# Eight PSUM banks shared out anew: a second score tile for the attention, two banks in place of three for the projections and for the values

## The chip, the cores and the metric

The kernel runs on one core of a Trainium2 chip. The metric is the device time of one execution in microseconds (us). The kernel before took 1664.14 us (median of 3 runs, 1662.96 to 1664.4).

## The reference

One layer of a hybrid decoder on a sequence of 1024 positions with 1024 channels, in float32:

```
z = x @ w_in; u, xl, gl, q, k, v, fg, gate_logits = split(z)
y_s5  = S5 branch of u        (32 groups of 64 complex states, a scan over the sequence, a gate)
y_lru = gelu(gl) * RG-LRU(conv4(xl))                                 (a scan over the sequence)
y_fox = softmax(q k^T / 8 + cum_i - cum_j, causal) v   (8 heads of 64; cum: sum of log forget gates)
x = LN(ALPHA * x + (sum_b sigmoid(gate_b) * (y_b @ w_branch_b)) @ w_out)
x = LN(ALPHA * x + (silu(x @ w_gate) * (x @ w_up)) @ w_down)
```

## The kernel before, in words

A float32 product is made of three matmuls of split operands (a high and a low part, `mm3` at line 119): high by high, high by low, low by high. A projection block of 128 channels by 512 positions is 24 matmuls of 512 columns into one bank of PSUM (`zpart`, line 194).

PSUM has eight banks of 2 KB a partition. Up to the end of the mixing stage one pool holds them, by tag. Tag `b`: one bank a tile, for the projection blocks and the short products of the S5 and LRU branches. Tag `a`: one bank a tile, for the attention's values (the output `po` of two query blocks and the transposed weights `ta`). Tag `s`: two banks a tile, for the scores of one query block against up to 1024 keys (`wide`, line 113). The start, the merge of the branches, the output projection and the transposes behind it take `a` and `b` by turns. After that the pool is closed and the feed-forward stage uses all eight banks as `p`.

Three streams are written one into another: `fox` (projections of q, k, v for a pair of heads, then their attention), `others` (the remaining projections, then the merges) and `side` (the S5 branch in four quarters, then the LRU branch). A scheduler then sets the order of each engine's instructions when the program is built, by its own model of durations and by which buffers are free. The engines run that order as it stands, each one strictly in turn.

The attention's step for head `hd` and query block `i` is `weights` (line 306): four or eight matmuls make the scores `s`; VectorE (DVE) adds the bias of the diagonal block (line 320, input `ndk`) and of the older blocks (line 323, input `nck`) and takes the row minimum, which also frees `s`; ScalarE (ACT) takes the exponential (line 324); DVE divides by the sum (lines 325 and 133). `values` (line 329) transposes these weights by PE (line 341), splits them on ACT and DVE (`tr`, lines 343 and 129), and multiplies them by the values.

At a head's first step the bias tiles are made (`head_bias`, line 299): `nck` is one DMA that spreads a head's row over all partitions, `ndk` is made of it on GpSimd (POOL, line 303). Each has one buffer, so that the DMA for a head waits for the last line 323 of the head before.

A projection block's bank is freed by its sink. For q that is two instructions on ACT and two on DVE (lines 389 to 392 of `q_sink`), for k two on ACT and four on DVE, for v a copy and then a second bank for the transposes; the other projections need one ACT instruction (`zs`).

At the end of the mixing stage, `mix_out` adds a block of 128 rows, `norm` (line 925) normalizes it on DVE, and `turn` (line 976) transposes it on PE for the feed-forward stage.

Of the kernel before, what the change touches and what calls it, by code (L numbers as in the profile page):

```python
# [13 lines left out]
F32 = mybir.dt.float32  # L14
# [7 lines left out]
P = 128  # L22
# [35 lines left out]
def trunk(ctx: ExitStack, tc: tile.TileContext, A: dict, out: bass.AP):  # L58
# [9 lines left out]
    psum = psum_stack.enter_context(tc.tile_pool(name="psum", bufs=1, space=PSUM))  # L68
# [18 lines left out]
    def name(n):  # L87
        count[0] += 1
        return f"{n}{count[0]}"
# [18 lines left out]
        return pools["side"].tile(list(shape), dt, name=name("sc"), tag="sc", bufs=8)  # L108

    def bank(shape=(P, 512), tag="b"):  # L110
        return psum.tile(list(shape), F32, name=name(tag), tag=tag, bufs=3)

    def wide():
        return psum.tile([P, 1024], F32, name=name("s"), tag="s", bufs=1)

    def mm(o, a, b, first, last):
        PE.matmul(o, a, b, start=first, stop=last)  # L117
# [61 lines left out]
    def load_x(tb):  # L179
        h, c = tb // 4, slice((tb % 4) * P, (tb % 4 + 1) * P)  # L180
        xt = new("s")
        SP.dma_start(xt, x_in[tb * P : (tb + 1) * P, :])
        for kp in range(4):
            if tb % 4 == 0:
                XH[h][kp] = new("x", F32R, (P, 2, 512))
                XL[h][kp] = new("m", F32R, (P, 2, 512))
            pa = bank([P, 2, P], "ab"[kp % 2])
            for kk in range(2):
                k = 2 * kp + kk
                PE.transpose(pa[:, kk, :], xt[:, k * P : (k + 1) * P], ident)  # L190
            ACT.copy(XH[h][kp][:, :, c], pa)
            tt(DVE, XL[h][kp][:, :, c], pa, XH[h][kp][:, :, c].bitcast(F32), ALU.subtract)

    def zpart(w, h, sink):
        ps = bank()
        for k in range(NK):
            mm3(ps, w[0][:, k, :], w[1][:, k, :], xh(h, k), xl(h, k), k == 0, k == NK - 1)
        sink(h, ps)
# [55 lines left out]
    def forget_sums():  # L254
# [4 lines left out]
        ACT.copy(wf, st)  # L259
        tt(DVE, wf[:, :, HEADS : 2 * HEADS], st[:, :, 0:HEADS], wf[:, :, 0:HEADS].bitcast(F32), ALU.subtract)  # L260
        pt_ = bank([P, NT, 2, HEADS], "a")
        for h in range(2):
            ps = bank()
# [42 lines left out]
    def weights(hd, i, qk, bias):  # L306


        qs, k1, k2 = qk
        nck, ndk = bias  # L310
        n = (i + 1) * P
        blk = slice(i * P, n)
        pt = new("pt")
        ps = wide()
        for c0 in range(0, n, 512):
            c = slice(c0, min(c0 + 512, n))
            mm(ps[:, c], qs[:, blk], k1[:, c], True, False)
            mm(ps[:, c], qs[:, blk], k2[:, c], False, True)
        md, m, l, rl = [few(f"st{e}", [P, 16], 4, "fox")[:, 0:1] for e in range(4)]
        DVE.tensor_tensor_reduce(out=pt[:, blk], in0=ps[:, blk], in1=ndk[:, i, :], scale=1.0, scalar=3.0e38, op0=ALU.add, op1=ALU.min, accum_out=md)  # L320
        if i:
            old = slice(0, i * P)
            DVE.tensor_tensor_reduce(out=pt[:, old], in0=ps[:, old], in1=nck[:, 0:i, :].rearrange("p t c -> p (t c)"), scale=1.0, scalar=md, op0=ALU.add, op1=ALU.min, accum_out=m)
        ACT.activation(pt[:, 0:n], pt[:, 0:n], AF.Exp, bias=m if i else md, scale=-1.0, accum_out=l)
        DVE.reciprocal(rl, l)
        ts(DVE, pt[:, 0:n], pt[:, 0:n], rl, ALU.mult)
        return pt
# [546 lines left out]
    while streams:  # L874
        s = min(streams, key=lambda e: e[0])
# [472 lines left out]
```

## Time and profile before

| | |
|---|---|
| runs | 1662.96, 1664.14, 1664.4 us |
| profiled execution | 1665.8 us, span 1664.1 us |
| PE busy | 1600.4 us (96%) |
| DVE, ACT, POOL busy | 1010.8, 633.9, 600.7 us |
| share of PE in the chain that ended last | 77% |

A PE that is busy all the time sets the end, so the profile is read by PE's idle stretches and by what ended them: the chain of waits and the table of waits name the releaser, the timeline shows the place. In the timeline and the tables a name stands without its number (`s<-q,q` are score matmuls); in the rows of the order the number tells one tile from another.

### The profile page before, as it was taken

Reading aid. Unit: us, or ns where it says so; the run is one execution under the profiler, and the core shown is the slowest. Engines: PE = TensorE matmul, PEld = TensorE weight load, DVE = VectorE, ACT = ScalarE, POOL = GpSimd, SP = SyncE. Lnnn points to the kernel's source line nnn. Section 1 sums busy time; section 2 is a strip of 40 time slices with the busy share of each in tenths; the row PEclk is TensorE's granted clock in tenths of the full one; section 3 lists DMA queues with packets and bytes.
Section 4 is the critical chain, followed back from the end, with each engine's and each line's share of the span. In section 5 each row is a group of like instructions: output and inputs, shape, how many; then the busy total and the mean of one; then the engine's idle time right before and its main releaser. Section 6 shows DMA issues by size and latency. Waiting matters only on the chain.

```text
span 1664.1 us, 20521 instructions
## 1 busy us (share of the span) xinstructions
PE 1600.4 (96%) x7482; PEld 1326.4 (80%) x7482; DVE 1010.8 (61%) x1602; ACT 633.9 (38%) x960; POOL 600.7 (36%) x529
## 2 busy tenths in 40 slices
PE   8989998999989999999999998999999999999997
PEld 6877887877877888888888886888888888778886
DVE  4746575633643366967758659675555555546766
ACT  4324454433543354656213224222222222244442
POOL 0111314442234011111140017599988788500004
PEclk9999999999989999999999998999999999999999
DMA  5332233333233334335654812356544445597752
GB/s 167 75 89 72 70 91 89 93 73 95 84 74 89 97 108 143 104 120 196 220 175 155 274 51 80 123 178 202 180 162 165 165 155 175 200 336 234 243 176 101
DMA packets 219968, 236.09 MB, mean 142 GB/s; under 512 B 33376, under 2 KB 162524, under 8 KB 219868
## 3 DMA queue, kind: packets, MB, share of 16 engines
q1 hardware_dynamic: 192604, 202.83, 39.1%
q10 hardware_dynamic: 27264, 31.96, 5.9%
q8 instruction: 59, 0.97, 0.2%
q14 instruction: 41, 0.34, 0.1%
HBM read 163.96 MB, written 70.78 MB: 141 GB/s over the span
## 4 chain that ended last, share of the span: by engine, by line
PE 77%; DVE 8%; DMA 5%; issue 4%; POOL 3%; ACT 2%; SPq 1%; ACTq 0%; DVEq 0%; POOLq 0%
PE p L117 34%; PE b L117 33%; PE a L117 8%; DMA nck<-ck_d 2%; PE s L117 2%; POOL s L129 1%; PE a L341 1%; DMA ws<-w_ffn_down 1%; DVE r L129 1%; DVE s L129 1%; POOL ln L129 1%; DVE wl L129 1%; DVE m L129 1%; ACT r L1235 1%; DMA row<-ln_b 1%
## 5 line engine op out<-in xcount | busy, mean ns | idle before, releaser
L117 PE MATMUL b<-x,wh 128*128 128x512 f32 x912 | 353.6, 399 | 2.3 <-ACT s L706 1.7
L117 PE MATMUL b<-x,wl 128*128 128x512 f32 x832 | 330.0, 397 | 0.0
L117 PE MATMUL b<-m,wh 128*128 128x512 f32 x784 | 310.8, 396 | 0.0
L117 PE MATMUL p<-mx,w 128*128 128x512 f32 x1056 | 250.5, 392 | 1.8 <-DVE mx L129 1.0
L117 PEld LDWEIGHTS p<-mx,w 128*128 128x128 f32 x1056 | 200.0, 190 | 44.3 <-POOL m L129 1.4
L117 PEld LDWEIGHTS b<-x,wh 128*128 128x128 f32 x912 | 173.9, 191 | 37.1 <-ACT s L706 2.0
L117 PEld LDWEIGHTS b<-x,wl 128*128 128x128 f32 x832 | 158.3, 190 | 32.4
L129 DVE TENSOR_TENSOR x<-x,p 128x512 f32<-128x512 f32 x163 | 108.4, 683 | 109.6 <-PE p L117 92.7
L117 PEld LDWEIGHTS b<-m,wh 128*128 128x128 f32 x784 | 149.9, 191 | 29.1 <-issue 0.2
L117 PE MATMUL p<-w,w 128*128 128x512 f32 x528 | 157.5, 390 | 1.2 <-DVE w L129 1.0
L129 POOL TENSOR_TENSOR s<-s,s 128x1024 f32<-128x1024 f32 (+9 forms) x76 | 77.5, 1020 | 207.4 <-ACT s L850 73.8
L129 DVE TENSOR_TENSOR w<-ws,w 128x1024 fp32r<-128x1024 f32 x88 | 115.3, 1316 | 52.7 <-ACT w L143 52.5
L143 ACT CAST w<-ws 128x1024 fp32r<-128x1024 f32 x88 | 92.1, 1050 | 110.5 <-PE p L117 72.6
L117 PE MATMUL p<-wo,w 128*128 128x512 f32 x528 | 127.3, 389 | 0.0
L129 DVE TENSOR_TENSOR wl<-ws,wh 128x1024 fp32r<-128x1024 f32 x62 | 85.3, 1376 | 65.7 <-ACT wh L143 62.4
L117 PEld LDWEIGHTS p<-w,w 128*128 128x128 f32 x528 | 98.8, 188 | 23.3 <-DVE w L129 2.9
L117 PEld LDWEIGHTS p<-wo,w 128*128 128x128 f32 x528 | 99.1, 188 | 20.6
L143 ACT CAST wh<-ws 128x1024 fp32r<-128x1024 f32 x62 | 65.1, 1050 | 125.1 <-PE b L117 94.4
L129 DVE TENSOR_TENSOR w<-m,w 128x1024 fp32r<-128x1024 f32 x44 | 67.6, 1536 | 63.5 <-ACT w L143 63.5
L129 POOL TENSOR_TENSOR ln<-x,x 128x512 f32<-128x512 f32 x44 | 75.7, 1726 | 64.0 <-ACT x L1170 52.6
L117 PE MATMUL p<-w 128*128 128x512 f32 x264 | 97.5, 390 | 1.1 <-ACT w L143 1.1
L129 POOL TENSOR_TENSOR r<-r,row 128x1024 f32<-128x1024 f32 x7 | 16.7, 2389 | 189.9 <-DVE r L129 184.7
(276 smaller groups left out, 2730.0 us busy)
## 6 DMA issues: line engine op xcount, KB each, us to landing
ws<-w_in SPq DMA_DIRECT2D x48, 512.0 KB, 4.5
ws<-w_ffn_gate SPq DMA_DIRECT2D x27, 512.0 KB, 4.5
gate_d<-zs ACTq DMA_DIRECT2D x48, 256.0 KB, 2.0
zs<-gate_d SPq DMA_DIRECT2D x48, 256.0 KB, 2.6
ws<-w_ffn_up SPq DMA_DIRECT2D x22, 512.0 KB, 4.7
x<-w_ffn_down SPq DMA_DIRECT2D x22, 512.0 KB, 5.5
hid_d<-ln SPq DMA_DIRECT2D x22, 512.0 KB, 4.2
wts_d<-x SPq DMA_DIRECT2D x22, 512.0 KB, 2.6
```

Source lines behind the costliest of these rows:

```text
L117: PE.matmul(o, a, b, start=first, stop=last)
L129: return pin(e.tensor_tensor(o, a, b, op))
L143: pin(ACT.copy(hi, src))
L341: PE.transpose(ta[:, j, e, :], pts[e][:, (k0 + j) * P : (k0 + j + 1) * P], ident)
L1235: pin(ACT.activation(r, r, AF.Identity, bias=nm, scale=rs))
```

## The change

The pool's counts: tags `a` and `b` go from three banks to two each, `s` from one tile of two banks to two tiles. The sum stays eight.

```diff
     def bank(shape=(P, 512), tag="b"):
-        return psum.tile(list(shape), F32, name=name(tag), tag=tag, bufs=3)
+        return psum.tile(list(shape), F32, name=name(tag), tag=tag, bufs=2)

     def wide():
-        return psum.tile([P, 1024], F32, name=name("s"), tag="s", bufs=1)
+        return psum.tile([P, 1024], F32, name=name("s"), tag="s", bufs=2)
```

No instruction is added or removed. The scheduler sees other buffers free, and the order of nearly every engine changes up to the end of the mixing stage. Three places follow.

PE where the sixth head (head 5) begins. `s_4134` are the last scores of head 4, `s_4197`, `s_4271` and `s_4374` the first three of head 5; `b_4214` and `b_4242` are projection blocks of 24 matmuls; `a_4320` are transposes of the weights that come out of `s_4134`. Before:

```order
L117 MATMUL s_4134<-q_3262,q_3258 128x512
L117 MATMUL a_4148<-tr_4150,q_3264 128x256 x4
...
L117 MATMUL s_4197<-q_3261,q_3259 128x128
L117 MATMUL s_4197<-q_3263,q_3259 128x128
L117 MATMUL a_4148<-tr_4170,q_3265 128x128
L341 MATMUL a_4328<-ident_77,pt_4118 128x128
L341 MATMUL a_4320<-ident_77,pt_4133 128x128
...
L117 MATMUL s_4271<-q_3261,q_3259 128x256
L117 MATMUL s_4271<-q_3263,q_3259 128x256
```

Now:

```order
L117 MATMUL s_4134<-q_3262,q_3258 128x512
L117 MATMUL b_4077<-s_3770,s_3664 128x128 x4
L117 MATMUL b_4214<-x_104,wh_4210 128x512
...
L117 MATMUL s_4197<-q_3261,q_3259 128x128
L117 MATMUL s_4197<-q_3263,q_3259 128x128
...
L117 MATMUL b_4242<-x_206,wh_4210 128x512
...
L117 MATMUL s_4271<-q_3261,q_3259 128x256
L117 MATMUL s_4271<-q_3263,q_3259 128x256
...
L117 MATMUL s_4374<-q_3261,q_3259 128x384
```

Two projection blocks now stand between the scores of head 4 and the second scores of head 5, and the transposes `a_4320` have moved behind the third scores.

DVE in head 1, where the q sink of the next pair of heads frees the banks `b_1861` and `b_1890`. `s_1415` and `s_1430` are the scores of query blocks 6 and 7, `s_1370` those of block 5. Before:

```order
L320 ISA pt_1414,st_1420<-s_1415,ndk_1164 128x128
...
L320 ISA pt_1429,st_1435<-s_1430,ndk_1164 128x128
...
L323 ISA pt_1429,st_1436<-s_1430,nck_1163,st_1435 128x896
...
L137 SCALAR_TENSOR_TENSOR q_1692<-b_1861,q_1692 64x512
...
L137 SCALAR_TENSOR_TENSOR q_1693<-b_1890,q_1693 64x512
```

Now:

```order
L320 ISA pt_1369,st_1375<-s_1370,ndk_1164 128x128
...
L129 TENSOR_TENSOR ho_1244<-a_1194,ho_1244 64x256
L129 TENSOR_TENSOR tr_1276<-a_1275,tr_1276 128x256
L323 ISA pt_1292,st_1299<-s_1293,nck_1163,st_1298 128x512
...
L323 ISA pt_1369,st_1376<-s_1370,nck_1163,st_1375 128x640
...
L133 TENSOR_SCALAR pt_1369<-pt_1369,st_1378 128x768
L137 SCALAR_TENSOR_TENSOR q_1692<-b_1861,q_1692 64x512
L137 SCALAR_TENSOR_TENSOR q_1693<-b_1861,q_1693 64x512
L137 SCALAR_TENSOR_TENSOR q_1692<-b_1890,q_1692 64x512
L137 SCALAR_TENSOR_TENSOR q_1693<-b_1890,q_1693 64x512
L129 TENSOR_TENSOR ho_1288<-a_1274,ho_1288 64x256
```

The four q instructions have moved from behind the scores of block 7 to between those of blocks 5 and 6. The bank of `b_1890` goes to the short product `b_1933` next, which stands on PE after the scores of block 7.

DVE at the end of the mixing stage. `x_8423` is row block 6, whose `norm` ends with the last row here; `wo_8613` and `wo_8609` are splits for the feed-forward stage. Before:

```order
L137 SCALAR_TENSOR_TENSOR x_8423<-x_8423,b_8628 128x512
L129 TENSOR_TENSOR x_8416<-x_8416,b_8665 128x512
L923 BN_STATS bn_8451<-x_8423 128x6
L928 BN_AGGR mv_8655<-bn_8451 128x2
L137 SCALAR_TENSOR_TENSOR x_8423<-x_8423,mv_8655,ln_8009 128x512 x2
L129 TENSOR_TENSOR wo_8613<-x_8416,wo_8612 128x4x128
L129 TENSOR_TENSOR wo_8609<-x_8675,wo_8608 128x4x128
L932 RECIPROCAL rs_8656<-rs_8656 128x1
L137 SCALAR_TENSOR_TENSOR x_8423<-x_8423,rs_8656,ln_8011 128x512 x2
```

Now:

```order
L137 SCALAR_TENSOR_TENSOR x_8423<-x_8423,b_8628 128x512
L923 BN_STATS bn_8451<-x_8423 128x6
L928 BN_AGGR mv_8655<-bn_8451 128x2
L137 SCALAR_TENSOR_TENSOR x_8423<-x_8423,mv_8655,ln_8009 128x512 x2
L932 RECIPROCAL rs_8656<-rs_8656 128x1
L129 TENSOR_TENSOR x_8416<-x_8416,b_8665 128x512
L137 SCALAR_TENSOR_TENSOR x_8423<-x_8423,rs_8656,ln_8011 128x512 x2
```

The two splits have moved behind the norm; on PE the transposes `b_8665` that `x_8416` needs stand 14 matmuls later.

## Rows read from the trace of the kernel before

**Rows 1.** The page: busy time by engine, granted clock in 40 slices.

```profile
PE 1600.4 (96%) x7482; PEld 1326.4 (80%) x7482; DVE 1010.8 (61%) x1602; ACT 633.9 (38%) x960; POOL 600.7 (36%) x529
...
PEclk9999999999989999999999998999999999999999
```

**Rows 2.** Table of waits, PE: waiter, releaser, total us, times, longest.

```profile
PE s L117 <- DVE st L320: 13.0, 4, 5.4
...
PE a L341 <- DVE pt L133: 3.6, 2, 3.2
...
PE s L117 <- DVE st L323: 2.3, 3, 1.0
...
PE b L117 <- ACT s L706: 1.7, 1, 1.7
```

**Rows 3.** Timeline of PE around head 5: start, us, count, wait.

```profile
447.30 1.17 PE L117 MATMUL s<-q,q 128*128 128x512 f32 x4
...
457.10 0.88 PE L341 MATMUL a<-ident,pt 128*128 128x128 f32 x6 [3.16 <-DVE pt L133]
463.40 0.80 PE L117 MATMUL s<-q,q 128*128 128x256 f32 x2 [5.43 <-DVE st L320]
...
464.07 0.78 PE L117 MATMUL b<-x,wh 128*128 128x512 f32 x1
...
468.48 0.41 PE L117 MATMUL b<-m,wh 128*128 128x512 f32 x1
```

**Rows 4.** Chain of waits in the same stretch: start, us, what.

```profile
451.30 1.06 DVE pt L323
...
452.39 9.41 DMA nck<-ck_d
...
461.93 1.09 POOL ndk L303
...
463.05 0.29 DVE pt L320
```

**Rows 5.** Timeline of PE at the starts of heads 0, 1 and 3.

```profile
120.14 0.62 PE L117 MATMUL s<-q,q 128*128 128x256 f32 x2 [2.89 <-DVE st L320]
...
147.74 1.18 PE L117 MATMUL s<-q,q 128*128 128x512 f32 x4 [0.47 <-DVE st L323]
...
162.15 0.51 PE L117 MATMUL s<-q,q 128*128 128x256 f32 x2 [1.54 <-DVE st L320]
...
263.92 1.07 PE L117 MATMUL s<-q,q 128*128 128x512 f32 x4
...
280.57 0.62 PE L117 MATMUL s<-q,q 128*128 128x256 f32 x2 [3.17 <-DVE st L320]
```

**Rows 6.** By stretch: length, busy us and count by engine, granted clock, DMA.

```profile
900.00:950.00 50.00, 50.00 (x223) 41.39 (x222) 34.37 (x50) 13.44 (x17) 0.00 (x0) 1.00 0.75 240
457.00:470.00 13.00, 7.47 (x26) 6.01 (x27) 5.66 (x16) 4.78 (x10) 7.84 (x10) 0.61 0.44 80
```

**Rows 7.** Timeline of DVE, then PE, at the end of the mixing stage.

```profile
1004.04 2.79 DVE L137 SCALAR_TENSOR_TENSOR x<-x,mv,ln 128x512 f32<-128x512 f32 x2
1006.75 3.42 DVE L129 TENSOR_TENSOR wo<-x,wo 128x512 fp32r<-128x512 f32 x2
...
1010.28 3.24 DVE L137 SCALAR_TENSOR_TENSOR x<-x,rs,ln 128x512 f32<-128x512 f32 x2
...
1011.94 1.09 PE L982 MATMUL b<-ident,x 128*128 128x128 f32 x4 [5.78 <-issue]
```

**Rows 8.** Groups by shape, DVE, 120 to 720 us: busy us, mean ns, idle before.

```profile
L320 DVE CUSTOM_DVE_ANT_0 pt<-s,ndk 128x128 f32<-128x128 f32 x64 | 18.3, 286 | 85.4 <-PE s L117 51.3 <-POOL ndk L303 27.3 <-PE a L341 6.6
...
L137 DVE SCALAR_TENSOR_TENSOR q<-b,q 64x512 fp32r<-64x512 f32 x12 | 8.3, 689 | 13.3 <-ACT q L390 13.1
...
L323 DVE CUSTOM_DVE_ANT_0 pt<-s,nck,st 128x640 f32<-128x640 f32 x8 | 7.0, 880 | 0.2
...
L133 DVE TENSOR_SCALAR pt<-pt,st 128x768 f32<-128x768 f32 x8 | 5.8, 719 | 0.2
```

## Prediction, made before the changed kernel ran

> **What bounds the kernel now.** I read the page first: PE is busy for 96% of the span and its granted clock is under nine tenths in two slices of forty only [rows 1]. PE is the bound, and no instruction of it is added or taken away. So the time can move only by PE's idle stretches and by what PE loses at the lower clock behind them. The second view is the table of PE's waits [rows 2], by releaser. The largest entry is `s<-q,q` waiting for line 320: four waits, 13.0 us together. The single score tile is not free, because the DVE instruction that reads it has not run. Beside it stand 2.3 us behind line 323 (the same tile, read by the second pass), 3.6 us for transposes that wait for the weights, and only 1.7 us on a `b` tile whose bank ACT had not yet freed.
>
> The timeline shows the largest of these at head 5 [rows 3]: after the last scores of head 4 (447.30, ended at 448.47) PE waits 3.16 us for a set of weights and then 5.43 us before the second scores of head 5. The chain of waits tells why [rows 4]: line 323 of the last block ends at 452.36, only then may the DMA of `nck` start (9.41 us), then POOL makes `ndk` (1.09 us), and at 463.05 line 320 reads the first scores. DVE and PE both stand still. The three other waits of the four are the starts of heads 0, 1 and 3: 2.89, 1.54 and 3.17 us [rows 5].
>
> **What the change gives.** With two score tiles the second scores of a head no longer need line 320 of the first; the third scores do. What counts is the PE work between the last scores of a head and the third scores of the next, against the time that DMA, POOL and DVE need.
>
> Head 5: needed are 463.34 - 448.47 = 14.9 us [rows 3, 4]. In the new order 48 matmuls of 512 columns stand between, at 50 us / 223 = 0.224 us each [rows 6], 10.8 us, and 52 small ones at 0.1 to 0.12 us (six in 0.88 us with the drain of the last [rows 3]), 5 to 6 us: about 16. The 5.43 us go. The 3.16 us go too: the transposes that waited stand behind the third scores now. Heads 1 and 3, counted in the same way: needed 162.15 - 148.92 = 13.2 and 280.57 - 264.99 = 15.6 us [rows 5]; the new order has about 13.9 and 15.5. Both waits go or leave some tenths: 1.54 + 3.17. Head 0 gains nothing: both its first score tiles are filled early, and its third scores then wait for the same line 320 at about the same place (2.89 us stay).
>
> Behind the wait at head 5 the clock is granted at 0.61 in the mean of 457 to 470 us [rows 6], and ten matmuls of 512 columns take 468.48 - 464.07 = 4.41 us instead of 2.24 [rows 3]: 2.1 us that go with the wait. Of the waits behind line 323 (2.3 us) I take 1 us as gained; they come again where the new order puts scores of two blocks side by side.
>
> The end of the mixing stage: PE waits 5.78 us for the norm of row block 6 [rows 7]. Before, DVE had two splits in the midst of that norm, 3.42 us; now they come behind it, while one smaller addition (0.6 us, as the distance of neighbouring rows of that size) has moved in. 2.8 us of the wait go. The splits are for products that come some tens of matmuls later, so nothing new is late. If the moved transposes `b_8665` (14 matmuls, 3.1 us later) should hold up the addition, the gain is nothing; below that it can't fall, since the end of the norm then waits as long as before.
>
> Sum of gains: 5.43 + 3.16 + 1.54 + 3.17 + 2.1 + 1.0 + 2.8 = 19.2 us.
>
> **What the change costs.** No wait before shows what two `b` banks do, so this is bounded. A projection block takes 24 x 0.224 = 5.4 us, so with three banks a sink may be 10.8 us late before PE stops, with two 5.4. Sinks of one ACT instruction stay far inside it. The sinks of q and k need DVE, and there DVE is the queue that holds them up.
>
> Head 1 is the clearest place. From line 320 on the scores of block 5 to the fourth q instruction DVE has: line 320 at 0.29, two passes of line 323 at up to 0.88, two of line 133 at 0.72, four q instructions at 0.69 [rows 8], three copies and additions of the values at an estimated 0.4: 0.29 + 1.76 + 1.44 + 2.76 + 1.2 = 7.5 us, some 0.07 less for each pair of neighbours, so about 6.5. PE has, from the end of these scores to the short product that takes over the q block's bank, eight score matmuls of 384 or 512 columns (1.7 us) and some 18 small ones (1.8 us): 3.5. PE must stand about 3 us. Before, the q instructions stood behind the scores of block 7, and the bank was not asked for until 25 us later. By the same count two more sinks are short by about 2.6 us each: that of k for the second pair of heads and that of q for the third. Together 8.2 us. Two places where an ACT sink frees a bank for the next short product of the S5 branch come out at 1.0 and 1.1 us. The start, where the transposes of x go through four banks in place of six, I take at 1 us; DVE limits it already. For the values (`a`), `po` holds one bank, so each set of transposes waits for the set before it to be split; other matmuls stand between in the new order, and I take nothing.
>
> Sum of costs: 8.2 + 2.1 + 1.0 = 11.3 us. Below, it can be nothing, if DVE runs ahead of this count. Above: each of the twelve q and k banks of the three later pairs short by 3 us, 36 + 3.1 = 39 us. I take the counted value, since the rows that it is made of are those of the instructions themselves.
>
> The clock may add to it. After the wait of 5.43 us the rows show 2.1 us lost at the lower clock [rows 3, 6]; the new waits are shorter, and I put nothing in the sum. [...]
>
> **The sum.** Against the profiled execution (1665.8 us, 1.7 above the median of the runs): 1665.8 - 19.2 + 11.3 = 1657.9; beside the median of 1664.1 that is 1656. A difference under 0.2% (3.3 us) I count as none, about what a measurement of this kernel can tell.
>
> **The rivals.**
> - Two banks are enough. For it: ACT's lateness on `b` shows in a single wait of 1.7 us [rows 2], and all sinks together leave PE hardly idle. Then the costs are nothing, and the time is 1664.1 - 19.2 = 1645. Against it: DVE's counts above. [...]
> - Slower: the sinks of q and k become a steady wait, at all twelve banks of the later pairs, 3 us each. For it: the scores of two blocks now come side by side, so DVE has two blocks' passes ahead of a sink. Then 1664.1 - 19.2 + 39 = 1684. It decides from a cost of 19 us on, about six such waits.
> - Slower: the wait moves instead of going. The DMA of `nck` still starts only after line 323 of the last block, and if line 323 comes later than now, because two blocks' passes arrive at once, the third scores wait as the second did. Then 10.1 + 3.2 + 2.1 us of the gains are lost: 1664.1 - 3.8 + 11.3 = 1672. Against it: the counts at heads 1, 3 and 5 meet what is needed, at head 5 with a microsecond to spare.
>
> **How the numbers follow.** Forecast 0.42 (its own range 1648 to 1663), two banks are enough 0.23, sinks 0.20, moved wait 0.15. Faster by over 0.2%: 0.33 of the forecast's share and all of the first rival, 0.56. Slower: 0.17 of the sinks' share, 0.13 of the moved wait's, 0.02 of the forecast's, 0.32. The same: the rest, 0.12. The range goes from 1638 (the first rival with what the clock and line 323 give back in full, and some luck) to 1684, the sinks' case at its price.
>
> **What would show it.** Right: in the waits of PE `s` behind line 320 falls from 13.0 to about 3 us with one wait left at head 0; the wait for line 133 falls under 1 us; the wait of line 982 is near 3 us; new waits of 2 to 3 us stand before short `b` products, released by DVE's line 137 or 129 on q, between 150 and 400 us. Wrong: `s` still waits 10 us behind line 320 (moved), no `b` waits at all (first rival), or more than 19 us of them; and most of all, losses on `a`, where I put nothing.

## The result, and the profile after

The changed kernel takes 1684.2 us (median of 4 runs, 1680.81 to 1687.12), the kernel before 1663.55 us beside it (4 runs, 1661.52 to 1664.4): ratio 1.0123, interval 1.0109 to 1.0136. It is 20.7 us slower; the forecast was 8 us faster, and the range ended at 1684. The profiled execution has a span of 1680.8 us, 16.7 more than before.

The page of the changed kernel: busy time, instructions, granted clock in 40 slices.

```profile
PE 1608.1 (96%) x7482; PEld 1326.9 (79%) x7482; DVE 1004.1 (60%) x1602; ACT 633.0 (38%) x959; POOL 602.9 (36%) x529
...
PEclk9999989998999999999999999999999999999999
```

Against [rows 1] the work is the same and the clock of this execution no worse: two slices in forty are below nine tenths, as before, and the mean granted clock over the span is 0.986 (before 0.984). So what is added in it is stops: PE is idle for 72.7 us of the span, before for 63.7. PE's busy time also grew by 7.7 us, but that is no added work: the last matmul ahead of a stop counts 0.39 us (start 117.90, ahead of the stop at 121.82), where one with a neighbour behind it takes 0.23 (117.67 to 117.90), so by estimate each further stop adds some 0.16 us of busy time.

PE's waits in the changed kernel, as [rows 2]: waiter, releaser, total us, times, longest.

```profile
PE a L341 <- DVE ho L129: 9.3, 2, 8.9
...
PE b L117 <- DVE s L129: 4.9, 4, 3.5
PE b L679 <- DMA nat<-s_c_re: 4.4, 2, 2.3
PE b L117 <- DVE q L137: 4.0, 3, 2.1
PE a L117 <- DVE tr L129: 3.9, 3, 2.0
PE s L117 <- DVE st L320: 3.8, 2, 3.5
PE p L117 <- DVE x L137: 3.2, 1, 3.2
...
PE b L117 <- DVE m L129: 2.0, 1, 2.0
...
PE b L982 <- DVE x L137: 0.5, 1, 0.5
```

The scores' wait fell from 13.0 to 3.8 us, as forecast, and nearly all that is left is one wait of 3.5 us at head 0. In its place stand waits on `b` and on `a`. The table misses short stops, so I also added up, for all PE instructions, the time from one start to the next beyond the shortest distance of that shape at the full clock (stops under 0.15 us left out), by the tile that came late:

| lost, us | before | after | difference | forecast |
|---|---|---|---|---|
| scores `s`, attention | 20.6 | 7.3 | -13.3 | -11.1 |
| values and transposes `a`, attention | 18.6 | 28.8 | +10.2 | -3.2 |
| projections and short products `b`, attention | 26.9 | 45.8 | +18.9 | +10.3, and -2.1 by the clock |
| start | 3.5 | 5.8 | +2.3 | +1.0 |
| end of the mixing stage | 11.8 | 7.3 | -4.5 | -2.8 |

That is +13.6 of the span's +16.7; the rest was not traced to a place. The sizes hang on what is taken as the shortest distance: with the median distance of each shape in its place the five differences are -10.6, +10.0, +13.7, +2.3 and -4.0. The signs hold by either count, the sizes to some 3 to 5 us.

The largest stop of all, on PE and then on the engine that it waits for (start, us, count, wait in brackets):

```profile
214.31 0.62 PE L341 MATMUL a<-ident,pt 128*128 128x128 f32 x4
223.80 1.11 PE L341 MATMUL a<-ident,pt 128*128 128x128 f32 x4 [8.87 <-DVE ho L129]
```

```profile
211.68 0.29 DVE L129 TENSOR_TENSOR tr<-a,tr 128x128 fp32r<-128x128 f32 x1 [0.33 <-ACT tr L343]
219.81 0.69 DVE L742 COPY s<-eab 128x1024 f32<-128x1024 f32 x1 [7.84 <-POOL s L129]
220.58 0.07 DVE L743 MEMSET s<- 128x8 f32 x1
220.65 1.23 DVE L129 TENSOR_TENSOR wl<-ws,wh 128x1024 fp32r<-128x1024 f32 x1
...
223.33 0.42 DVE L129 TENSOR_TENSOR ho<-a,ho 64x256 f32<-64x256 f32 x1
```

DVE stands still for 7.84 us: line 742 fills a tile of the S5 branch that POOL still uses. Behind it in DVE's order is the instruction that reads `po` and so frees a bank of `a` (`ho`), and PE's next transposes need that bank. POOL is late because it had itself stood, in the midst of its work on that tile, for the bias of the next head:

```profile
200.73 1.09 POOL L303 TENSOR_SCALAR_AFFINE_SELECT ndk<-nck 128x1024 f32<-128x1024 f32 x1 [10.43 <-DMA nck<-ck_d]
```

These 10.43 us are more than the 7.84 for which DVE waits; by estimate, without them it would not have waited. In the kernel before PE doesn't stop at this place, but the same fill in a later quarter (PE at 531.90) cost it 3.2 us:

```profile
PE a L117 <- DVE s L743: 3.2, 1, 3.2
```

I had read past it. The largest stop on `b` is inside the S5 branch (PE, POOL and DVE by time, and the last ACT instruction that makes an operand):

```profile
468.04 1.05 ACT L761 COPY s<-s 64x1024 f32<-64x1024 f32 x1
...
471.20 0.39 PE L117 MATMUL b<-s,s 128*128 128x128 f32 x2
471.29 1.09 POOL L303 TENSOR_SCALAR_AFFINE_SELECT ndk<-nck 128x1024 f32<-128x1024 f32 x1 [19.15 <-DMA nck<-ck_d]
471.42 0.60 PE L341 MATMUL a<-ident,pt 128*128 128x128 f32 x4
471.78 0.72 PE L117 MATMUL a<-tr,q 128*128 128x256 f32 x4
472.35 2.33 POOL L129 TENSOR_TENSOR s<-s,s 128x1016 f32<-128x1016 f32 x1
474.72 1.22 DVE L129 TENSOR_TENSOR s<-s,s 128x1016 f32<-128x1016 f32 x1 [3.90 <-POOL s L129]
...
475.99 4.38 PE L117 MATMUL b<-s,s 128*128 128x128 f32 x24 [3.49 <-DVE s L129]
```

The short product opens its bank at 471.20 with an operand that is ready and waits for the second one (`hh`, made on POOL and DVE) until 475.99; the bank stays taken all that time. One bank is left for projections, and PE's order has none to put there. What PE waits for here is the operand, not a bank. And the operand is late by the bias again: ACT had its part ready at 469.09, but POOL, in its order, first waited for the DMA of `nck` and made `ndk`, until 472.35. These 3.3 us are nearly the whole of PE's 3.49.

A projection that does wait for a bank stands at 413.89 (PE, ACT and DVE by time, rows left out):

```profile
411.42 0.66 PE L705 MATMUL b<-ident,s 128*128 128x128 f32 x4 [0.98 <-ACT s L706]
...
411.58 1.28 ACT L324 ACT_TABLE_LOAD   x1
...
413.27 0.56 ACT L706 COPY s<-b 128x512 f32<-128x512 f32 x1
413.63 1.41 DVE L129 TENSOR_TENSOR q<-b,q 64x512 fp32r<-64x512 f32 x2
413.89 0.80 PE L117 MATMUL b<-x,wh 128*128 128x512 f32 x1 [1.82 <-ACT s L706]
```

One bank is with a k block, whose sink on DVE ends at 415.04; the other is with a short product that is complete at 412.08 and is copied out by ACT (line 706) only behind other work.

The waits that I had forecast are there too, one for the head 1 place and one for the third pair of heads, and smaller:

```profile
185.92 1.03 PE L117 MATMUL b<-s,s 128*16 128x128 f32 x8 [1.55 <-DVE q L137]
...
382.60 0.30 PE L679 MATMUL b<-ident,nat 128*128 128x128 f32 x1 [2.33 <-DMA nat<-s_c_re]
385.02 0.78 PE L117 MATMUL b<-x,wh 128*128 128x512 f32 x1 [2.11 <-DVE q L137]
```

### The profile page after: what moved, and what is told of

It is laid out like the page before. It is cut to its first block, busy times and chain, and to the rows that moved or that the text cites. A ratio compares the mean times of both kernels' runs of the same rounds, so it can differ in the third digit from the quotient of the medians.

```text
span 1680.8 us, 20491 instructions
## 1 busy us (share of the span) xinstructions
PE 1608.1 (96%) x7482; PEld 1326.9 (79%) x7482; DVE 1004.1 (60%) x1602; ACT 633.0 (38%) x959; POOL 602.9 (36%) x529
## 4 chain that ended last, share of the span: by engine, by line
PE 63%; DVE 5%; DMA 3%; ACT 2%; POOL 2%; issue 1%; SPq 0%; DVEq 0%; ACTq 0%; POOLq 0%
PE p L117 32%; PE b L117 23%; PE a L117 7%; DMA ws<-w_ffn_down 1%; POOL s L129 1%; DMA nck<-ck_d 1%; DVE r L129 1%; DVE x L137 1%; PE s L117 1%; PE a L341 1%; DVE wo L129 1%; ACT r L1235 1%; DMA s<-gl_d 1%; DMA row<-ln_b 0%; DVE bn L923 0%
## 5 line engine op out<-in xcount | busy, mean ns | idle before, releaser
L117 PEld LDWEIGHTS p<-mx,w 128*128 128x128 f32 x1056 | 199.4, 189 | 45.8 <-DVE x L137 3.5
L129 DVE TENSOR_TENSOR wl<-ws,wh 128x1024 fp32r<-128x1024 f32 x62 | 81.8, 1319 | 95.0 <-ACT wh L143 81.7
L117 PEld LDWEIGHTS p<-wo,w 128*128 128x128 f32 x528 | 99.1, 188 | 20.6
L129 DVE TENSOR_TENSOR tr<-a,tr 128x512 fp32r<-128x512 f32 (+2 forms) x112 | 55.2, 494 | 57.2 <-ACT tr L343 57.0
```

Of the source, the lines that this page charges most:

```text
L129: return pin(e.tensor_tensor(o, a, b, op))
```

## The experiments

Twelve kernels ran, each with the kernel before on the same chip. Ratios are to that, with their 95% intervals.

**Which bank costs.** One score tile as before, and the counts alone:

```diff
-        return psum.tile(list(shape), F32, name=name(tag), tag=tag, bufs=3)
+        return psum.tile(list(shape), F32, name=name(tag), tag=tag, bufs={"a": 2, "b": 2}[tag])
```

> One score tile as before, and both cuts: two banks each for b and a (six of eight banks used). Theory 'banks': the cuts cost what they cost in the changed kernel (PE's waits on b from 27 to 46 us, on a from 19 to 29 us, start-to-start against the pitch at full rate), and the 13 us that the second score tile gave back are missing: 1690 to 1700 us, with PE waiting some 13 us or more for line 320. Theory 'order': what moved the time is which order the scheduler happened to write, and the number of banks hardly counts: anywhere from 1655 to 1685, not above the changed kernel.

Measured: 1685.66 us, 1.015 (1.0135 to 1.0166).

With `{"a": 2, "b": 3}`:

> One score tile, two banks for a, three for b. Theory 'banks': only the loss on a (some 10 us) remains: 1670 to 1678 us, PE's waits on b near those of the kernel before. Rival: b alone is what costs, and a is free (as the prediction took it): 1660 to 1667. Theory 'order': no telling, 1655 to 1685.

Measured: 1660.63 us, 0.9996 (0.9987 to 1.0006).

With `{"a": 3, "b": 2}`:

> One score tile, three banks for a, two for b. Theory 'banks': the loss on b (some 19 us, and 2 us at the start) remains: 1680 to 1690 us. Rival, a alone costs: 1660 to 1667. Theory 'order': no telling, 1655 to 1685, and not ranked as e2 below e3 below e1.

Measured: 1679.52 us, 1.012 (1.0099 to 1.0141).

With `{"a": 2, "b": 4}`:

> One score tile, two banks for a, four for b. Since the third bank of a was worth nothing and the third of b some 19 us: a fourth of b gains a little more, 1652 to 1660 us, if b is still short at three; the same as the kernel before within 3 us, if three are enough.

Measured: 1657.97 us, 0.9982 (0.997 to 0.9994).

Of these expectations e2's rival holds (`b` alone costs); e1 and e3 came out just below the ranges for the banks. With one score tile, the third bank of `a` is worth nothing beside three banks of `b`, and some 6 us beside two (e3 against e1, whose intervals just overlap). The third bank of `b` is worth 18.5 us with three banks for `a` and 25.0 with two; the fourth some 2, inside the intervals. So `b` is the cost. And e1 against the changed kernel (1.015 against 1.0123, the intervals just overlap) prices the second score tile: by itself it brings some 4 us, though it takes 17 us from the losses of `s` (24.4 in e1 by the same sum as in the table, 7.3 in the changed kernel; 12.6 us by the median count). The losses of `a` are 17.9 in e1 and 28.8 in the changed kernel: 11 us come back there, and most of that is the one stop of 8.87 us, which e1 doesn't have.

**Who holds `b`.** Tags `a` and `b` two banks each, one score tile, and the two banks that are left as a tag `c` for the short products of the S5 and LRU branches (seven calls like this one, the gates' groups of 12 and of 3 matmuls of 512 columns among them):

```diff
-            py = bank([P, 4, P])
+            py = bank([P, 4, P], "c")
```

> One score tile, two banks for a, two for b as in e1, and two banks of their own (tag c) for the short products of the S5 and LRU branches, eight in all. Theory 'short products': what two b banks cost is that a short product that waits for DVE, ACT or a DMA keeps one of them, so that projection blocks run on a single bank; with banks of their own the loss goes: 1657 to 1668 us. Rival 'sinks' (the prediction's): the sinks of q and k themselves are too slow for two banks, whoever else uses them: 1675 to 1688, near e1 and e3.

Measured: 1661.68 us, 0.9994 (0.9981 to 1.0008).

The projections have two banks here as in e1, with the same sinks of q and k, and the 25 us are gone. These rows of its table of waits show what two banks cost then:

```profile
PE b L117 <- DVE q L129: 2.5, 4, 1.2
PE b L117 <- DVE m L129: 2.0, 1, 2.0
...
PE c L117 <- DVE s L129: 1.7, 2, 1.3
PE b L117 <- DVE q L137: 1.7, 1, 1.7
```

PE waits 4.2 us for the sinks of q and k in all (`q` at lines 129 and 137), not the 8.2 that I had put there nor the 36 of the rival; in the changed kernel the same two rows add up to 4.5. So the slow sinks are not what made two banks dear; the short products that share them are. Two things e5 leaves open. It gives the work of `b` four banks where e1 has two, so it doesn't tell how much is a short product that keeps its bank while it waits and how much is merely more products for two banks. And three shared banks (e2, 0.9996) do as well as two and two apart.

**The wait at 215 us.** The changed kernel, with the fill of lines 742 and 743 on POOL, behind the instruction that it waits for:

```diff
-        DVE.tensor_copy(r8, eab[:, 1, g8].unsqueeze(2).broadcast_to([P, 8, P]))
-        DVE.memset(r8[:, :, 0:1], 0.0)
+        with after(late_pool[0]):
+            POOL.tensor_copy(r8, eab[:, 1, g8].unsqueeze(2).broadcast_to([P, 8, P]))
+            POOL.memset(r8[:, :, 0:1], 0.0)
```

> The changed kernel with the S5 branch's fill of its decay tile (lines 742 and 743) moved from DVE to POOL, which makes the tile's data anyway; PE's order stays all but the same. Theory 'DVE is held up': the 8.9 us that PE stands at 215 us, because DVE waits 7.8 us for POOL at line 742 with the freeing of a bank of a behind it, go, and little else: 1672 to 1678 us. Rival, the wait only comes elsewhere (POOL becomes late for the next quarter, or another instruction in front of the same one is late): 1682 to 1687.

Measured: 1679.46 us, 1.0109 (1.0094 to 1.0124). PE's wait at that place, in its timeline:

```profile
219.36 1.12 PE L341 MATMUL a<-ident,pt 128*128 128x128 f32 x4 [3.53 <-DVE ho L129]
```

The time lies between the two ranges. 8.87 us became 3.53, but the ratio fell only from 1.0123 to 1.0109, within the intervals. So the largest single wait isn't the price of the change: `ho` stays late behind other DVE work, and of the 5.3 us saved there no more than some 2 show in the time.

**Is it an accident of the order?** One number of the scheduler's table, `T_FOX`, from 10.0 to 11.0, in the kernel before and in the changed one:

```diff
-T_FOX = 10.0
+T_FOX = 11.0
```

> The kernel before with one constant of the written order changed (T_FOX 10 to 11), no bank. It measures what another order alone does: PE's order differs in 2503 lines. Theory 'banks': within 5 us of the kernel before, 1656 to 1668. Theory 'order': 10 us or more away on either side.

Measured: 1652.87 us, 0.9947 (0.9929 to 0.9964).

> The changed kernel with the same constant changed (T_FOX 10 to 11). Theory 'banks': still slow, 1674 to 1690 us. Theory 'order': may fall to 1665 or below.

Measured: 1675.0 us, 1.008 (1.0057 to 1.0102).

The order alone moves the kernels by 7 to 9 us, by their ratios: more than theory 'banks' allowed for e6, less than theory 'order' asked. The change costs 22.1 us in this order (1675.0 - 1652.87) and 20.7 in the first, so in both orders that ran it is the banks. In e7 the losses of `b` are 37.2 (e6: 23.0), of `a` 28.4 (15.3), of `s` 7.3 (17.2): the same three shifts as in the table above (the profiled execution of e6, 1658.15 us, is the longest of its eight). The stop on `a` behind `ho` is there again, with 8.8 us.

**Can the score wait be had without `b`'s bank?** `b` keeps three, `a` has two, and query blocks 0 and 2 get a one-bank tile of their own:

```diff
-    def wide():
+    def wide(i):
+        if i in (0, 2):
+            return psum.tile([P, 512], F32, name=name("h"), tag="h", bufs=1)
...
-        ps = wide()
+        ps = wide(i)
```

> The second score tile in one bank instead of two: tag h, one tile of 512 columns, used by query blocks 0 and 2 of each head (their scores have at most 384 columns); all others keep the tile of two banks. Two banks for a, three for b: eight. Theory 'the second score tile is worth its 13 us where no bank of b pays for it': 1646 to 1654 us. Rival 'the score tile's wait is worth little, because DVE gives it back on the values' (e1 against the changed kernel: 4 us): 1656 to 1664, like e2.

Measured: 1654.03 us, 0.995 (0.9935 to 0.9965), at the upper end of the theory's range. Two lines are added ahead, so that line 320 is 322 here:

```profile
PE h L119 <- DVE st L322: 6.3, 3, 3.0
```

The wait for the bias moved to the new tile and is half of the 13.0.

> e9 with the constant of e6 (T_FOX 11), to see how much of e9 is order: against e6 (1652.9) some 10 us less if the second tile is worth that much in either order, 1640 to 1648; 1650 to 1658 if it is not.

Measured: 1655.01 us, 0.9953 (0.9937 to 0.9969); e6 has that order without the small tile and is at 0.9947. So in the other order the tile brings nothing (the second of the two ranges), and what it brought in the first can't be told from a better order.

**Or is the wait not PSUM's at all?** The kernel before, all its banks as they were, and two buffers in SBUF for each of the two bias tiles:

```diff
-        ... "nck": ("fox", 1), "ndk": ("fox", 1),
+        ... "nck": ("fox", 2), "ndk": ("fox", 2),
```

> The kernel before with two buffers each for the bias tiles nck and ndk, so that the DMA of a head's bias need not wait for the last block of the head before. If PE's wait for line 320 is the bias coming late, it goes by this without any bank: line 320 in the waits of PE falls from 13.0 to some 3 us (head 0 stays), and the time to 1648 to 1655 us. Rival: the order that comes out is another and hides it, 1656 to 1668.

Measured: 1644.92 us (1644.2 to 1645.28), 0.9893 (0.9876 to 0.9909): 17.4 us faster than before, faster than the range forecast, and the fastest of all. PE's waits:

```profile
PE s L117 <- DVE st L323: 3.2, 4, 1.0
...
PE s L117 <- DVE st L320: 2.4, 1, 2.4
```

And who waits for the bias of line 303, in the kernel before and then here:

```profile
  DVE pt L320: 27.3, 4
```

```profile
  DVE pt L320: 7.0, 1
```

Four waits of DVE for the bias became one, at head 0 (117.49), and PE's wait behind line 320 went from 13.0 to 2.4 us with a single score tile. The order changed throughout here too, and by e6 that alone can be some 9 us of the 17.4; the waits that went are the part that the rows show. The granted clock is part of it too: the median over e10's executions is 0.991, over those of the kernel before on the same chip 0.987, by estimate 7 us of a span of 1660. The second buffer was not tried in another order, and not in the changed kernel; so how much of that kernel's 20.7 us goes back to the late bias stays open, though it stands behind the stops at 223.80 and 475.99. By these rows the buffer that was short was that of the bias in SBUF; a PSUM tile only moved the wait (6.3 us on `h` in e9) or shortened it (13.0 to 3.8 us in the changed kernel).

Both together:

> The kernel before with two buffers each for nck and ndk (1644.92 us, ratio 0.989 in its own run) and, with them, the one-bank second tile for the scores of key blocks 0 and 2 (0.995 by itself). Theory: both remove the same wait, that of a head's first score multiplies for the bias row that a late DMA brings; with the bias row early the second tile has nothing left to save: ratio 0.987 to 0.992, 1641 to 1650 us, and the wait of score multiplies on VectorE's line 320 is at most 3 us in either. Rival: the tile saves its own wait, independent of the bias: the two add, ratio 0.984 or less, about 1637 us.

Measured: 1651.19 us, 0.9922 (0.9903 to 0.994). They don't add: with the bias early the small tile seems to cost some 5 us (0.9922 against 0.9893; the intervals just overlap). The ratio is at the far end of the theory's range, the time just outside it. Why it costs, and isn't merely idle, I have not settled; its order differs throughout.

## Why the prediction was wrong

The step that failed is "What the change costs". Its sum was 11.3 us; by the table `b` cost 18.9 (13.7 by the median count) and the start 2.3, and `a` 10.2, where the prediction has "I take nothing". It priced how long the sinks of q and k take; it did not price the short products that share the two banks, nor what else DVE, ACT and POOL are held up by.

- **The gain on the scores: right, by size and place.** In the table of waits lines 320 and 323 fall from 15.3 to 4.3 us, 11.0 less where 11.1 stood. Head 5's wait is gone, and one wait at head 0 remained, forecast as 2.9 and measured as 3.5. The moved-wait rival is refuted.
- **The transposes behind line 133 at head 5** (3.16 us) went, as forecast. But `a` as a whole lost 10.2. The prediction said of its two banks that "other matmuls stand between in the new order"; it counted PE's side and not DVE's, which has to free the bank. Most of the loss is the one stop at 223.80, in both orders: DVE held by POOL, and POOL by the DMA of the bias. That DVE can be held by POOL was written in a row of before that I did not use. Two banks of `a` cost nothing with one score tile and three banks of `b` (e2, 0.9996), and on `a` the second score tile goes with 11 us more (e1 against the changed kernel); so what I priced one by one was no sum of its parts. Whether DVE's passes over the scores of two blocks also make `tr` and `ho` late is not shown.
- **`b`: the wrong holder.** I asked how long a sink needs and took the slowest sinks, those of q and k. Their waits came at two of the three places (185.92, 385.02), with half the size, 4.0 us. The other stops on `b` stand at the short products themselves and at projections: PE's idle time before `b` in the attention grew from 7.7 to 20.5 us, by 8.2 before short products and by 4.3 before projections. A short product kept a bank for 4.8 us while its second operand was late (471.20 to 475.99), longer than the four q instructions on DVE take for two banks (2.83 us from 184.37), and "Sinks of one ACT instruction stay far inside it" did not hold where ACT was behind (1.82 us at 413.89). e5 shows that the sinks of q and k were not the price: with the short products elsewhere, two banks for the projections cost nothing.
- **The slower rival** (sinks of q and k at all twelve banks, 1684) has the measured time by luck: e5 has those sinks with two banks and loses nothing.
- **The first rival** (two banks are enough, 1645) falls with e1 (1.015) and e3 (1.012). The projections have two banks in e1 as in e5 (0.9994), so their number alone doesn't decide the time.
- **The clock: a small cost, put at nothing.** The 2.1 us behind head 5's wait were counted as a gain, what the new waits cost by it was not. In the profiled execution it fell behind the new stops and came back where the old ones had been, as these stretches of the changed kernel show (columns as in [rows 6]; the kernel before has a clock of 1.00 in the first and of 0.87 in the second, that of head 5, where [rows 6] has 0.61):

```profile
200.00:250.00 50.00, 39.35 (x203) 33.12 (x203) 24.93 (x65) 21.61 (x44) 18.18 (x33) 0.90 0.20 55
442.00:464.00 22.00, 22.00 (x115) 18.81 (x114) 13.40 (x30) 10.51 (x18) 9.83 (x9) 1.00 0.29 87
```

Over this span that evens out, 0.984 to 0.986. Over all executions it does not quite: the kernel before has 0.985 to 0.990 beside the experiments (median 0.987), the changed kernel 0.982 to 0.986 (median 0.985). That is 0.2%, by estimate 3 of the 20.7 us (0.002 of a span of 1664); the one profiled pair doesn't show it.
- **The end of the mixing stage**: -4.5 where -2.8 stood; the wait of line 982 fell from 5.8 to 0.5, and 3.2 came up at the feed-forward's first product. At the **start**, 2.3 where 1.0 stood.

The prediction also took the order for a given. e6 shows that a turn of one number in the scheduler is worth 9 us, as much as the whole forecast gain of 8.

## What to carry to other kernels

Before taking a bank from a tag, ask for each kind of product in it how long it keeps the bank from its first matmul to its last reader, waits for late operands and for the engine of the reader included (here 4.8 us at 471.20 and 1.8 us at 413.89). A count of the slowest sinks alone missed most of the price here. A tag of its own for the products that wait isn't cheaper as such: two banks and two did here what three shared ones did (e5 0.9994, e2 0.9996). Follow a wait on PSUM back past the instruction that frees it: here a late DMA into a single SBUF buffer stood behind it, and a second buffer there came out 17 us faster (a new order and the clock included), where a second PSUM tile gave 4 and the banks for it cost 25. And where a scheduler sets the order, run the change in a second order before a difference under a per cent is put down to it.

## What was not expected of the chip

Engines carried a wait on to work that has nothing to do with it: POOL's arithmetic for the S5 branch held DVE for 7.84 us at line 742, and through DVE the attention's transposes on PE for 8.87 us. POOL had before that stood for 10.43 us at another head's bias, whose DMA was late (issued at 191.32, behind the line 323 that ended at 191.25). So a single buffer in SBUF reached PE through the DMA, POOL and DVE, at a tile that has nothing to do with it.
